# A Strassen-type channel mixer: where its first operands lie, when the right token sums are made, and the order of its last products

## The chip, the cores and the metric

The kernel runs on one core of a Trainium2 chip. The metric is device microseconds (us) of one execution. Engines: PE multiplies matrices, DVE (VectorE), ACT (ScalarE) and POOL (GpSimd) work elementwise, SP issues every transfer of this kernel, in the order of its queue.

## The reference

One layer on 2048 latent tokens of 1024 channels, float32. Up to the middle it is a token mixer (a state-space scan and a pooling mixer, then an output projection); what changes lies behind it:

```
x  = x + mx[2] * rmsnorm(yx, post_norm_mix)
hx = modulate(rmsnorm(x, pre_norm_ffn), mx[3], mx[4])
up = dwconv3(hx @ w_up) ; v, g = split(up)          # 1024 -> 2 x 2816
x  = x + mx[5] * rmsnorm((silu(g) * v) @ w_down, post_norm_ffn)   # 2816 -> 1024
```

## The kernel before, in words

**Numbers.** Each float32 operand is split in two (`split`, lines 117 to 122: `hi` by a cast, line 119, mostly on ACT; `lo = x - hi` by a subtraction, line 122, on DVE or POOL), and each product is three matmuls (`mm3`, lines 150 to 152).

**Token mixer, last part** (lines 906 to 962). The output projection runs over four blocks of 512 tokens, from block 3 down to block 0. Each block takes two halves of the columns; a half needs four units of `w_out` (`wunit`, load at line 129, `lo` on POOL). `Post.half` (lines 810 to 816) squares on ACT (814) and multiplies by the gate row `cr` on DVE (816); `Post.finish` (818 to 836) works out the row scale (`rstd`, lines 154 to 166), loads the residual `xr` (828, two buffers), adds it (834) and stores x1 (836). Blocks 3 and 0 keep their rows in `XB`, blocks 2 and 1 in `eb`. `norm_x1` (880 to 896) then normalises blocks 3, 2 and 1 inside the next block's products and stores them transposed to `h_d` (895): blocks 3 and 2 make the right half of the tokens, `h_d[1]`. Block 0 is done later, by `norm_late`, inside the channel mixer.

**Up-projection** (lines 964 to 1174). It is a Strassen-Winograd product: seven products of quarter matrices in place of eight. `right_sums` (1006) loads four slices of `h_d[1]` (992), makes the sums T1 to T4 (1003) and splits all seven right operands (`xcB11`, `xcT2` and so on) slice by slice. `up_pair(1, i)`, 22 times, loads two units of `w_up` (`rawu`, 1052 and 1057, four buffers), makes weight sums in a buffer `st` (1060 to 1063, two buffers) and runs the products in the order B11, T2, T1, T3, B21, B22, T4, twelve matmuls each, with split weights `wo` (six buffers). Then come the left tokens (`left_sums`, `left_operand`, `up_pair(0, i)`), `act_sums` (sums of the activations, stored to `s_d`, 1146 and 1147) and `down_sums` (sums of `w_down` to `ds_d`).

**Down-projection** (lines 1179 to 1290). Again seven products, of eleven steps each. A step loads a stationary tile `ar` (1200), splits it into `as` (three buffers), loads a weight tile `rw` (1190), splits it into `tc`, and does 24 matmuls on eight banks `psf`. Order: 6, 5, 3, 1, 7, 2, then 4. The last one goes by rows j = 0 to 7, 33 matmuls each. `add` (1241) adds a bank into `accd`; `half_row` squares half a row (1230, ACT) and multiplies it by the gate (1231); `rows` (1211 to 1224) makes the row scales, loads the residual `xr` (1221, two buffers), adds it (1223) and stores the result (1224). Before the change `rows` of both token halves, th = 0 and 1, run inside the last product.

**What sets the order.** Nobody writes the queues by hand: a planner orders each engine's instructions ahead of time. An instruction's rank is its place in the code; `hot()` moves it 500 places ahead. Memory comes from pools that are stacked from the left or the right end and closed together: `sp` (left: `wdt`, `edge`, `tail`, `eb`, `xt`, `ef`, `CT`, `BT` and so on, `cr` near its end) and `main` (right) of the token mixer; `fx` (left) over `sp`, and `fst`, `frw`, `fwo`, `fu` (right) over `main`; at last `fd` (left), 207 KB a partition, over all of these. The channel mixer's pools are opened with `reuse_waits="tile"`.

Of the kernel before, what the change touches and what calls it, by code (L numbers as in the profile page):

```python
# [9 lines left out]
F32 = mybir.dt.float32  # L10
# [25 lines left out]
EPS = 1e-6  # L36


HOT, NW, NPRE, AHEAD, NU, NU2 = 500, 7, 7, 3, 4, 5

ORDER = "p3 c0 p2 c1 p1 b0 p0 b1 x0 x1 x3 x2".split()
ORDER_LAST = "c0 p3 c1 b0 b1 p2 x0 p1 x1 p0 x3 x2".split()
# [10 lines left out]
def hybrid_block(ctx: ExitStack, tc: tile.TileContext, x, cx, ccol, crow, par, rowpar, cst, edge,  # L53
# [3 lines left out]

    const = ctx.enter_context(tc.tile_pool(name="const", bufs=1))
    mctx = ExitStack()
    main = mctx.enter_context(tc.tile_pool(name="main", bufs=1, side="right"))  # L60
    psx, pools = [], {}

# [18 lines left out]
        return main.tile([P, n], F32, tag=name, name=name, bufs=bufs)  # L81

    def t512(dt=F32):
        return main.tile([P, 516], dt, tag="t512", name="t512", bufs=3)

    def cacc():
        return main.tile([P, TB], F32, tag="cacc", name="cacc", bufs=3)

    hxh = main.tile([P, KD, TB + 4], F32R, name="hxh")
    hxl = main.tile([P, KD, TB + 4], F32R, name="hxl")  # L90
# [15 lines left out]
    act_d = [[dp.tile([NK, P, 2 * TB], F32, name=f"act_d{kh}{th}") for th in range(2)] for kh in range(2)]  # L106
    s_d = [dp.tile([NK, P, 2 * TB], F32, name=f"s_d{n}") for n in range(1, 5)]

    hs_d = dp.tile([4, P, 4, TB], F32, name="hs_d")
    ds_d = dp.tile([NK, P, 4, 512], F32, name="ds_d")  # L110
    wu_d = [[dp.tile([P, 1024], F32, name=f"wu_d{m}_{s}") for s in range(4)] for m in range(NFF)]

# [185 lines left out]
    nc.sync.dma_start(out=edge_t, in_=edge.rearrange("g n -> (g n)").partition_broadcast(P))  # L298

    tail = stile([P, 8, 4], "tail")  # L300

    def conv(m, srcs, t, first, dest):


        c0 = 2 if first else 4
        raw = main.tile([P, TB + 4], F32, tag="raw", name="raw", bufs=2)
# [316 lines left out]
    adar = const.tile([P, 32], F32, name="adar")  # L623

    def ada_rest():
        cr = stile([P, D], "cr")
# [250 lines left out]

    A2, B2 = adar[:, 16:24], adar[:, 8:16]

    def norm_x1(ys, b):  # L880

        ss = small(4, "ss4")
        for i in range(4):
            S.activation(out=junk, in_=ys[i], func=AF.Square, accum_out=ss[:, i:i + 1])
        r = rstd(ss, 4, D)
        for i in range(4):
            V.tensor_scalar(out=ys[i], in0=ys[i], scalar1=r[:, i:i + 1], scalar2=None, op0=MUL)
        yield
# [28 lines left out]
    for b in range(NB - 1, -1, -1):  # L917
# [40 lines left out]
            pst.half(hh, po)  # L958
        run(ngen)
        pst.finish()  # L960
        if b:
            ngen = norm_x1(ys, b)
    sctx.close()
# [19 lines left out]
    def four():  # L983
        return fst.tile([P, 4, 512], F32, tag="st", name="st", bufs=2)

    def wide(tag, bufs):
        return main.tile([P, 2 * TB + 4], F32, tag=tag, name=tag, bufs=bufs)

    def quarters_of(p, kk):
        hb = four()  # L990
        for h in range(2):
            nc.sync.dma_start(out=hb[:, 2 * h:2 * h + 2, :],
                              in_=h_d[p][kk + 4 * h].rearrange("p (t c) -> p t c", t=2))
        return hb

    def quarter_sums(hb, put):

        b11, b12, b21, b22 = (hb[:, q_, :] for q_ in range(4))
        for n, s_ in (("B11", b11), ("B21", b21), ("B22", b22)):
            put(n, s_)  # L1000
        for n, o_, x_, y_ in (("T1", b11, b12, b11), ("T3", b12, b22, b12), ("T2", b22, b22, b11),
                              ("T4", b21, b21, b22)):
            V.tensor_tensor(out=o_, in0=x_, in1=y_, op=SUB)  # L1003
            put(n, o_)

    def right_sums():
        for kk in range(4):
            def put(n, s_):
                split(xc[n][:, kk, :], xc[n][:, 4 + kk, :], s_, S, V)
            quarter_sums(quarters_of(1, kk), put)  # L1010

    def left_sums(kk):
        hb = quarters_of(0, kk)
        quarter_sums(hb, lambda n, s_: None)
        nc.sync.dma_start(out=hs_d[:, :, kk, :].rearrange("s p c -> p s c"), in_=hb)

    def left_operand(n):
        hb = four()
        if n in ("T1", "T3", "T4", "T2"):
            src = hs_d[("T1", "T3", "T4", "T2").index(n)]  # L1020
        else:
            h, t = int(n[1]) - 1, int(n[2]) - 1
            src = h_d[0][4 * h:4 * h + 4, :, t * TB:(t + 1) * TB].rearrange("k p c -> p k c")
        nc.sync.dma_start(out=hb, in_=src)
        for h in (0, 2):
            split(xc[n][:, h:h + 2, :], xc[n][:, 4 + h:6 + h, :], hb[:, h:h + 2, :], S, V)

# [127 lines left out]
            V.tensor_tensor(out=o_, in0=x_, in1=y_, op=SUB)  # L1155
        nc.sync.dma_start(out=ds_d[k], in_=t)

    right_sums()
    side = []
    for i in range(4):  # L1160
        side += [norm_late(i)] * 2
    for n_, i in enumerate(j + h * NK for j in range(NK) for h in range(2)):
# [1 line left out]
        if 1 <= n_ <= 8:  # L1164
            next(side[n_ - 1])
        if n_ in (12, 14, 16, 18):
            left_sums(n_ // 2 - 6)
    for n in NAMES:
        left_operand(n)
    for k in range(NK):  # L1170
        vs = [up_pair(0, k)]
        down_sums(k)
# [13 lines left out]
    def weights(n, k):  # L1186

        src = (ds_d if n > 3 else w_down)[k][:, {1: 0, 2: 2, 3: 3, 5: 0, 7: 1, 4: 2, 6: 3}[n], :]
        t = main.tile([P, 512], F32, tag="rw", name="rw", bufs=3)
        nc.sync.dma_start(out=t, in_=src)  # L1190
        tc_ = main.tile([P, 1024], F32R, tag="tc", name="tc", bufs=12)
        split(tc_[:, 0:512], tc_[:, 512:1024], t, S, V)
        return tc_[:, 0:512], tc_[:, 512:1024]

    STAT = {6: s_d[1], 5: s_d[0], 3: s_d[3], 1: act_d[0][0], 7: s_d[2], 2: act_d[1][0], 4: act_d[1][1]}

    def product(n, o, start, stop):
        for k in range(NK):
            t = main.tile([P, 2 * TB], F32, tag="ar", name="ar", bufs=3)
            nc.sync.dma_start(out=t, in_=STAT[n][k])  # L1200
            a = main.tile([P, 2, 2 * TB], F32R, tag="as", name="as", bufs=3)
            split(a[:, 0], a[:, 1], t, S, V)
            w = weights(n, k)
            for j in range(8):
                js = slice(j * P, (j + 1) * P)
# [5 lines left out]
    def rows(th, js):  # L1211
# [49 lines left out]
    product(2, o, True, True)  # L1261
    for j in range(8):
        add(c11, j)
    for j in range(8):
        half_row(3, j)

    tw = [weights(4, k) for k in range(NK)]
    for j in range(8):
        t = main.tile([P, NK, P], F32, tag="ra", name="ra", bufs=2)
        nc.sync.dma_start(out=t, in_=STAT[4][:, :, j * P:(j + 1) * P].rearrange("k p t -> p k t"))  # L1270
        so = main.tile([P, 2, NK, P], F32R, tag="so", name="so", bufs=2)
        split(so[:, 0], so[:, 1], t, S, V)
        if j == 0:
            o = banks()
        for k in range(NK):
            mm3(o[j], (so[:, 0, k, :], so[:, 1, k, :]), tw[k], k == 0, k == NK - 1)
        add(c21, j)
        half_row(2, j)
        if j < 7:
            half_row(0, j)  # L1280
            half_row(1, j)
        if j in (3, 5, 6, 7):
            js = {3: (0, 1, 2, 3), 5: (4, 5), 6: (6,), 7: (7,)}[j]
            rows(1, js)
            if j < 7:
                rows(0, js)
            if j == 6:
                half_row(0, 7)
                half_row(1, 7)
                rows(0, (7,))  # L1290


def _layout(inp):
# [69 lines left out]
```

## Time and profile before

| | us |
|---|---|
| median of 3 runs (lowest, highest) | 2325.04 (2323.08, 2328.54) |
| the profiled execution's own time | 2326.06 |
| its span | 2323.7 |
| PE busy in the span | 2115.2 (91%) |
| DVE, ACT, POOL busy | 1639.1, 904.4, 449.1 |

In time lines the columns are start, duration, engine, source line, operation, output<-input, count and, in brackets, the engine's idle time before it and what ended it. "x2" is two instructions in one row. PEclk 1.00 is full clock (2.4 GHz), 0.50 is 1.2 GHz.

### The profile page before, as it was taken

Reading aid. Unit: us, or ns where it says so; the run is one execution under the profiler, and the core shown is the slowest. Engines: PE = TensorE matmul, PEld = TensorE weight load, DVE = VectorE, ACT = ScalarE, POOL = GpSimd, SP = SyncE. Lnnn points to the kernel's source line nnn. Section 1 sums busy time; section 2 is a strip of 40 time slices with the busy share of each in tenths; the row PEclk is TensorE's granted clock in tenths of the full one; section 3 lists DMA queues with packets and bytes.
Section 4 is the critical chain, followed back from the end, with each engine's and each line's share of the span. In section 5 each row is a group of like instructions: output and inputs, shape, how many; then the busy total and the mean of one; then the engine's idle time right before and its main releaser. Section 6 shows DMA issues by size and latency. Waiting matters only on the chain.

```text
span 2323.7 us, 27270 instructions
## 1 busy us (share of the span) xinstructions
PE 2115.2 (91%) x9473; PEld 1680.8 (72%) x9473; DVE 1639.1 (71%) x2504; ACT 904.4 (39%) x1386; POOL 449.1 (19%) x553
## 2 busy tenths in 40 slices
PE   8788999799789889399999999999999789999994
PEld 4686777687457667188888888877888668888883
DVE  5778868967678565788878888877776643334546
ACT  4434433333324544445544445333333243333331
POOL 1533513525356433000001001100000000000000
PEclk9889999899799889599999999999999989999997
DMA  7757969859765654555576659998867494444417
GB/s 299 269 180 240 310 224 343 271 203 287 243 231 161 221 175 163 212 204 199 209 253 225 248 214 334 384 375 322 281 229 281 156 313 158 147 140 148 141 53 273
DMA packets 238698, 541.37 MB, mean 233 GB/s; under 512 B 52000, under 2 KB 100832, under 8 KB 234720
## 3 DMA queue, kind: packets, MB, share of 16 engines
q1 hardware_dynamic: 238560, 539.64, 66.4%
q8 instruction: 74, 1.21, 0.2%
q14 instruction: 64, 0.52, 0.1%
HBM read 362.22 MB, written 177.34 MB: 232 GB/s over the span
## 4 chain that ended last, share of the span: by engine, by line
PE 53%; DVE 2%; DMA 2%; issue 1%; ACT 1%; SPq 0%; POOL 0%; ACTq 0%; POOLq 0%; DVEq 0%
PE pu L150 12%; PE pu L151 12%; PE pu L152 12%; PE psf L150 6%; PE psf L151 6%; PE psf L152 6%; DMA xr<-x_d 1%; DVE accd L1223 0%; DMA st<-h_d 0%; DVE xcB L122 0%; DMA xr<-in_x_dram 0%; DMA ar<-s_d 0%; DVE st L1003 0%; DVE xcT L122 0%; DVE XB L834 0%
## 5 line engine op out<-in xcount | busy, mean ns | idle before, releaser
L150 PE MATMUL pu<-xcT,wo 128*128 128x512 f32 x704 | 278.4, 396 | 1.3 <-ACT wo L119 1.3
L151 PE MATMUL pu<-xcT,wo 128*128 128x512 f32 x704 | 278.5, 396 | 0.0
L152 PE MATMUL pu<-xcT,wo 128*128 128x512 f32 x704 | 276.9, 394 | 0.0
L150 PE MATMUL pu<-xcB,wo 128*128 128x512 f32 x528 | 210.7, 400 | 40.1 <-ACT xcB L119 36.5
L150 PE MATMUL psf<-tc,as 128*128 128x512 f32 x528 | 204.8, 393 | 21.3 <-ACT tc L119 21.3
L122 DVE TENSOR_TENSOR as<-ar,as 128x1024 fp32r<-128x1024 f32 x66 | 80.8, 1224 | 197.5 <-ACT as L119 197.4
L151 PE MATMUL pu<-xcB,wo 128*128 128x512 f32 x528 | 210.9, 399 | 1.3 <-DVE xcB L122 1.3
L152 PE MATMUL pu<-xcB,wo 128*128 128x512 f32 x528 | 208.6, 398 | 0.0
L151 PE MATMUL psf<-tc,as 128*128 128x512 f32 x528 | 205.7, 389 | 0.0
L152 PE MATMUL psf<-tc,as 128*128 128x512 f32 x528 | 203.1, 389 | 0.0
L150 PE MATMUL pu<-wh,hxh 128*128 128x512 f32 x384 | 157.3, 422 | 23.5 <-DVE eb L816 7.4
L152 PE MATMUL pu<-hxh,wl 128*128 128x512 f32 (+2 forms) x448 | 164.9, 371 | 2.9 <-POOL wl L122 2.0
L150 PE MATMUL pu<-hxh,wh 128*128 128x512 f32 (+2 forms) x448 | 164.8, 373 | 2.0 <-ACT wh L119 1.4
L151 PE MATMUL pu<-hxl,wh 128*128 128x512 f32 (+2 forms) x448 | 166.0, 371 | 0.0
L151 PE MATMUL pu<-wl,hxh 128*128 128x512 f32 x384 | 159.6, 416 | 6.0 <-POOL wl L122 6.0
L122 POOL TENSOR_TENSOR wl<-wst,wh 128x1024 fp32r<-128x1024 f32 x48 | 120.9, 2518 | 217.5 <-ACT wh L119 201.6
L150 PEld LDWEIGHTS pu<-xcT,wo 128*128 128x128 f32 x704 | 132.6, 188 | 33.1 <-ACT wo L119 1.6
L151 PEld LDWEIGHTS pu<-xcT,wo 128*128 128x128 f32 x704 | 132.7, 188 | 31.2
L152 PEld LDWEIGHTS pu<-xcT,wo 128*128 128x128 f32 x704 | 132.4, 188 | 31.1
L119 ACT CAST wo<-rawu 128x512 fp32r<-128x512 f32 x132 | 81.7, 620 | 187.8 <-PE pu L152 168.1
L152 PE MATMUL pu<-wh,hxl 128*128 128x512 f32 x384 | 153.8, 409 | 0.0
L119 ACT CAST as<-ar 128x1024 fp32r<-128x1024 f32 x66 | 69.6, 1054 | 210.4 <-PE psf L152 185.9
(325 smaller groups left out, 4594.6 us busy)
## 6 DMA issues: line engine op xcount, KB each, us to landing
wu_d<-wo SPq DMA_DIRECT2D x88, 512.0 KB, 2.8
wo<-wu_d SPq DMA_DIRECT2D x88, 512.0 KB, 5.7
rawu<-in_w_up_dram SPq DMA_DIRECT2D x66, 512.0 KB, 4.2
wh<-wk_d SPq DMA_DIRECT2D x48, 512.0 KB, 6.7
wl<-wk_d SPq DMA_DIRECT2D x48, 512.0 KB, 6.1
ar<-s_d SPq DMA_DIRECT2D x44, 512.0 KB, 3.4
XB<-in_w_ada_b_dram SPq DMA_DIRECT2D x32, 512.0 KB, 6.7
wst<-in_w_out_dram SPq DMA_DIRECT2D x32, 512.0 KB, 4.4
```

Source lines behind the costliest of these rows:

```text
L119: S.copy(out=hi, in_=src)
L122: le.tensor_tensor(out=lo, in0=src, in1=hi.bitcast(F32), op=ALU.subtract)
L150: PE.matmul(o, lt[0], rt[0], start=start, stop=False, **kw)
L151: PE.matmul(o, lt[0], rt[1], start=False, stop=False, **kw)
L152: PE.matmul(o, lt[1], rt[0], start=False, stop=stop, **kw)
```

## The change

- A new pool `top`, the outermost on the right, takes `t512`, `cacc` and `raw` out of `main`; `frw` (the `rawu` buffers) is the first pool opened on the right afterwards and so lies over `top`. `fst` is gone: its two `st` buffers lie in `fx`. `cr` becomes the fourth tile of `sp`.
- In `fx` the places are given in a new order: B21 and T3 first (over `cr`, `eb`, `xt`), then `st`, then B11, T2, T1. B22 joins T4 in `fu`.
- The quarter sums of the right tokens are made behind block 1 of the output projection, in `XB`, and stored to `hs_d[1]`. The right operands are then loaded whole (1 MB each), as the left ones were, five of them with priority 2000.
- Loads and splits of the down-projection become `hot`; `as` gets two buffers, over the places of B21, allocated ahead of `ar`; its `xr` gets four.
- The products end in the order 6, 5, 3, 2, 1, 7, 4. `half_row` and `rows` for th = 0 move ahead of the adds behind product 7; product 4 keeps those of th = 1.

```diff
@@ pools
-HOT, NW, NPRE, AHEAD, NU, NU2 = 500, 7, 7, 3, 4, 5
+HOT, EARLY, NW, NPRE, AHEAD, NU, NU2 = 500, 2000, 7, 7, 3, 4, 5
+    top = mctx.enter_context(tc.tile_pool(name="top", bufs=1, side="right"))
     main = mctx.enter_context(tc.tile_pool(name="main", bufs=1, side="right"))
...
-        return main.tile([P, 516], dt, tag="t512", name="t512", bufs=3)
+        return top.tile([P, 516], dt, tag="t512", name="t512", bufs=3)
...
-    hs_d = dp.tile([4, P, 4, TB], F32, name="hs_d")
+    hs_d = [dp.tile([4, P, 4, TB], F32, name=f"hs_d{p}") for p in range(2)]
...
     tail = stile([P, 8, 4], "tail")
+    cr = stile([P, D], "cr")
@@ behind block 1
+    def quarter_sums(p, kk, hb):
+
+        for h in range(2):
+            nc.sync.dma_start(out=hb[:, 2 * h:2 * h + 2, :],
+                              in_=h_d[p][kk + 4 * h].rearrange("p (t c) -> p t c", t=2))
+        b11, b12, b21, b22 = (hb[:, q_, :] for q_ in range(4))
+        for o_, x_, y_ in ((b11, b12, b11), (b12, b22, b12), (b22, b22, b11), (b21, b21, b22)):
+            V.tensor_tensor(out=o_, in0=x_, in1=y_, op=SUB)
+        nc.sync.dma_start(out=hs_d[p][:, :, kk, :].rearrange("s p c -> p s c"), in_=hb)
...
         pst.finish()
+        if b == 1:
+            for kk in range(4):
+                quarter_sums(1, kk, XB[:, kk % 2 * 4 * TB:(kk % 2 + 1) * 4 * TB].rearrange("p (q c) -> p q c", q=4))
@@ up-projection
-    fx, fst, frw, fwo = (fpool(*a) for a in (("fx", "left"), ("fst", "right"), ("frw", "right"), ("fwo", "right")))
+    fx, frw, fwo = (fpool(*a) for a in (("fx", "left"), ("frw", "right"), ("fwo", "right")))
...
-    xc = {n: (main if n == "T4" else fx).tile([P, 8, TB], F32R, name="xc" + n) for n in NAMES}
+    def operand(n):
+        xc[n] = (main if n in ("B22", "T4") else fx).tile([P, 8, TB], F32R, name="xc" + n)
+
+    operand("B21")
+    operand("T3")
...
+    sts = [four(), four()]
+    for n in ("B11", "T2", "T1", "B22", "T4"):
+        operand(n)
...
-    def left_operand(n):
-        hb = four()
...
+    def load_operand(p, n):
+        hb = sts.pop() if sts else four()
...
-    right_sums()
+    with tc.high_priority(offset=EARLY):
+        for n in ("B11", "T2", "T1", "T3", "B21"):
+            load_operand(1, n)
+    for n in ("B22", "T4"):
+        load_operand(1, n)
@@ down-projection
-            t = main.tile([P, 2 * TB], F32, tag="ar", name="ar", bufs=3)
-            nc.sync.dma_start(out=t, in_=STAT[n][k])
-            a = main.tile([P, 2, 2 * TB], F32R, tag="as", name="as", bufs=3)
-            split(a[:, 0], a[:, 1], t, S, V)
+            with hot():
+                a = main.tile([P, 2, 2 * TB], F32R, tag="as", name="as", bufs=2)
+                t = main.tile([P, 2 * TB], F32, tag="ar", name="ar", bufs=3)
+                nc.sync.dma_start(out=t, in_=STAT[n][k])
+                split(a[:, 0], a[:, 1], t, S, V)
...
-            res = main.tile([P, D], F32, tag="xr", name="xr", bufs=2)
+            res = main.tile([P, D], F32, tag="xr", name="xr", bufs=4)
...
+    product(2, o, True, True)
+    for j in range(8):
+        S.copy(out=c11[j], in_=o[j])
+    o = banks()
     product(1, o, True, False)
     for j in range(8):
-        S.copy(out=c11[j], in_=o[j])
+        add(c11, j)
         add(c12, j)
     product(7, o, False, True)
+    for js in ((0, 1, 2, 3), (4, 5, 6, 7)):
+        for j in js:
+            half_row(0, j)
+            half_row(1, j)
+        rows(0, js)
     for j in range(8):
+        add(c22, j)
         add(c21, j)
-        add(c22, j)
-    o = banks()
-    product(2, o, True, True)
-    for j in range(8):
-        add(c11, j)
-    for j in range(8):
-        half_row(3, j)
...
             mm3(o[j], (so[:, 0, k, :], so[:, 1, k, :]), tw[k], k == 0, k == NK - 1)
+        half_row(3, j)
         add(c21, j)
         half_row(2, j)
-        if j < 7:
-            half_row(0, j)
-            half_row(1, j)
         if j in (3, 5, 6, 7):
-            js = {3: (0, 1, 2, 3), 5: (4, 5), 6: (6,), 7: (7,)}[j]
-            rows(1, js)
...
+            rows(1, {3: (0, 1, 2, 3), 5: (4, 5), 6: (6,), 7: (7,)}[j])
```

`weights` and the `ra`, `so` tiles of product 4 are put under `hot()` in the same way; `cacc` and `raw` move to `top` like `t512`; `quarter_sums(0, ..)` takes the place of `left_sums`, with the same work.

## Rows read from the trace of the kernel before

**Rows 1.** The page: PE's busy share in 40 slices of the span, in tenths.

```profile
PE   8788999799789889399999999999999789999994
```

**Rows 2.** Windows: stretch, length, busy us (instructions) by engine, PEclk, DMA share, GB/s.

```profile
860.00:900.00 40.00, 39.52 (x176) 31.63 (x175) 25.55 (x44) 22.06 (x41) 14.41 (x6) 1.00 0.56 196
950.00:984.50 34.50, 14.41 (x28) 7.20 (x29) 33.61 (x67) 23.39 (x44) 0.00 (x0) 0.50 0.37 132
1700.00:1800.00 100.00, 100.00 (x432) 80.79 (x431) 70.66 (x78) 31.97 (x40) 8.86 (x27) 1.00 0.76 271
2100.00:2200.00 100.00, 100.00 (x443) 82.81 (x442) 53.17 (x70) 38.02 (x61) 0.00 (x0) 1.00 0.43 143
```

**Rows 3.** Time line of PE: last matmul of block 0, first of the up-projection.

```profile
924.32 0.39 PE L152 MATMUL pu<-wh,hxl 128*128 128x512 f32 x1
949.86 0.79 PE L150 MATMUL pu<-xcB,wo 128*128 128x512 f32 x1 [25.16 <-ACT xcB L119]
```

**Rows 4.** Time line of SP ahead of and around the first handover.

```profile
851.05 6.88 SPq L895 DMA_DIRECT2D h_d<-t  x8
...
916.56 1.69 SPq L895 DMA_DIRECT2D h_d<-t  x2
...
936.81 2.80 SPq L836 DMA_DIRECT2D x_d<-XB  x2
939.71 0.37 SPq L1052 DMA_DIRECT2D rawu<-in_w_up_dram  x1
```

**Rows 5.** Time line of DVE ahead of and around the first handover.

```profile
897.72 0.68 DVE L816 TENSOR_TENSOR XB<-pu,cr 128x512 f32<-128x512 f32 x1
...
928.72 2.48 DVE L834 SCALAR_TENSOR_TENSOR XB<-XB,r,xr 128x1024 f32<-128x1024 f32 x2
...
937.98 1.28 DVE L834 SCALAR_TENSOR_TENSOR XB<-XB,r,xr 128x1024 f32<-128x1024 f32 x1 [1.19 <-DMA xr<-in_x_dram]
```

**Rows 6.** Time line of PE at the second handover.

```profile
1867.79 3.78 PE L150 MATMUL psf<-tc,as 128*128 128x512 f32 x8 [21.28 <-ACT tc L119]
```

**Rows 7.** Time line of SP around the second handover.

```profile
1835.20 19.33 SPq L1128 DMA_DIRECT2D act_d<-av  x2
...
1858.36 1.58 SPq L1147 DMA_DIRECT2D s_d<-av  x2
1860.03 0.58 SPq L1200 DMA_DIRECT2D ar<-s_d  x1
...
1869.51 4.57 SPq L1221 DMA_DIRECT2D xr<-x_d  x2
```

**Rows 8.** Time line: PE's last matmul and DVE's last addition.

```profile
2288.53 0.39 PE L152 MATMUL psf<-tc,so 128*128 128x512 f32 x1
...
2318.60 1.28 DVE L1223 SCALAR_TENSOR_TENSOR accd<-accd,r,xr 128x1024 f32<-128x1024 f32 x1 [2.48 <-DMA xr<-x_d]
```

**Rows 9.** DMA issues, whole span: count, KB each, median us from issue to landing.

```profile
ds_d<-st SPq DMA_DIRECT2D x11, 1024.0 KB, 8.4
...
st<-h_d SPq DMA_DIRECT2D x16, 512.0 KB, 5.1
...
out_dram<-accd SPq DMA_DIRECT2D x16, 512.0 KB, 3.4
```

**Rows 10.** Lines, 940 to 985 us: the sums of the right operands, busy us and mean ns.

```profile
L1003 DVE TENSOR_TENSOR st<-st 128x512 f32<-128x512 f32 x16 | 11.0, 686 | 0.1
```

**Rows 11.** What PE waited for, 690 to 925 us: total, times, longest.

```profile
PE pu L150 <- DVE eb L816: 7.4, 1, 7.4
```

**Rows 12.** Time line of POOL and DVE, 894 to 899 us.

```profile
895.19 2.39 POOL L122 TENSOR_TENSOR wl<-wst,wh 128x1024 fp32r<-128x1024 f32 x1 [5.74 <-PE pu L152]
...
895.35 2.25 DVE L163 TENSOR_TENSOR r<-r 128x4 f32<-128x4 f32 x1
```

**Rows 13.** The page: the split of a 128x1024 tile, `lo` on DVE and `hi` on ACT.

```profile
L122 DVE TENSOR_TENSOR as<-ar,as 128x1024 fp32r<-128x1024 f32 x66 | 80.8, 1224 | 197.5 <-ACT as L119 197.4
...
L119 ACT CAST as<-ar 128x1024 fp32r<-128x1024 f32 x66 | 69.6, 1054 | 210.4 <-PE psf L152 185.9
```

More of the change, by code (lines that the diff above doesn't have):

```diff
@@ L83, in t512 @@
     def t512(dt=F32):
-        return main.tile([P, 516], dt, tag="t512", name="t512", bufs=3)
+        return top.tile([P, 516], dt, tag="t512", name="t512", bufs=3)
     def cacc():
-        return main.tile([P, TB], F32, tag="cacc", name="cacc", bufs=3)
+        return top.tile([P, TB], F32, tag="cacc", name="cacc", bufs=3)
     hxh = main.tile([P, KD, TB + 4], F32R, name="hxh")
@@ L300, in hybrid_block @@
     tail = stile([P, 8, 4], "tail")
+    cr = stile([P, D], "cr")
     def conv(m, srcs, t, first, dest):
         c0 = 2 if first else 4
-        raw = main.tile([P, TB + 4], F32, tag="raw", name="raw", bufs=2)
+        raw = top.tile([P, TB + 4], F32, tag="raw", name="raw", bufs=2)
         if first:
@@ L625, in ada_rest @@
     def ada_rest():
-        cr = stile([P, D], "cr")
         junk2 = stile([P, D], "junk2", 1, BF16)
@@ L972, in fpool @@
         return at.enter_context(tc.tile_pool(name=name, bufs=1, side=side, reuse_waits="tile", **kw))
-    fx, fst, frw, fwo = (fpool(*a) for a in (("fx", "left"), ("fst", "right"), ("frw", "right"), ("fwo", "right")))
+    fx, frw, fwo = (fpool(*a) for a in (("fx", "left"), ("frw", "right"), ("fwo", "right")))
     main = fpool("fu", "right")
     NAMES = ("B11", "T2", "T1", "T3", "B21", "B22", "T4")
-    xc = {n: (main if n == "T4" else fx).tile([P, 8, TB], F32R, name="xc" + n) for n in NAMES}
+    xc = {}
@@ L980, in hybrid_block, with four @@
+    def operand(n):
+        xc[n] = (main if n in ("B22", "T4") else fx).tile([P, 8, TB], F32R, name="xc" + n)
+    operand("B21")
+    operand("T3")
+    def four():
+        return fx.tile([P, 4, 512], F32, tag="st", name="st", bufs=2)
+    sts = [four(), four()]
+    for n in ("B11", "T2", "T1", "B22", "T4"):
+        operand(n)
     sv = main.tile([P, 2 * NFF, 2], F32, name="sv")
     last = main.tile([P, NK], F32, name="last")
-    def four():
-        return fst.tile([P, 4, 512], F32, tag="st", name="st", bufs=2)
@@ L986, in wide @@
     def wide(tag, bufs):
         return main.tile([P, 2 * TB + 4], F32, tag=tag, name=tag, bufs=bufs)
-    def quarters_of(p, kk):
-        hb = four()
[L991 to L1015, printed above, removed]
-    def left_operand(n):
-        hb = four()
-        if n in ("T1", "T3", "T4", "T2"):
-            src = hs_d[("T1", "T3", "T4", "T2").index(n)]
+    def load_operand(p, n):
+        hb = sts.pop() if sts else four()
+        if n[0] == "T":
+            s_ = hs_d[p][("T1", "T3", "T4", "T2").index(n)]
@@ L1021, in left_operand @@
         else:
             h, t = int(n[1]) - 1, int(n[2]) - 1
-            src = h_d[0][4 * h:4 * h + 4, :, t * TB:(t + 1) * TB].rearrange("k p c -> p k c")
-        nc.sync.dma_start(out=hb, in_=src)
+            s_ = h_d[p][4 * h:4 * h + 4, :, t * TB:(t + 1) * TB].rearrange("k p c -> p k c")
+        nc.sync.dma_start(out=hb, in_=s_)
         for h in (0, 2):
@@ L1166, in hybrid_block @@
         if n_ in (12, 14, 16, 18):
-            left_sums(n_ // 2 - 6)
+            quarter_sums(0, n_ // 2 - 6, four())
     for n in NAMES:
-        left_operand(n)
+        load_operand(0, n)
     for k in range(NK):
@@ L1188, in weights @@
         src = (ds_d if n > 3 else w_down)[k][:, {1: 0, 2: 2, 3: 3, 5: 0, 7: 1, 4: 2, 6: 3}[n], :]
[L1189 to L1192, printed above, removed]
+        with hot():
+            t = main.tile([P, 512], F32, tag="rw", name="rw", bufs=3)
+            nc.sync.dma_start(out=t, in_=src)
+            tc_ = main.tile([P, 1024], F32R, tag="tc", name="tc", bufs=12)
+            split(tc_[:, 0:512], tc_[:, 512:1024], t, S, V)
         return tc_[:, 0:512], tc_[:, 512:1024]
@@ L1198, in product @@
         for k in range(NK):
-            t = main.tile([P, 2 * TB], F32, tag="ar", name="ar", bufs=3)
-            nc.sync.dma_start(out=t, in_=STAT[n][k])
-            a = main.tile([P, 2, 2 * TB], F32R, tag="as", name="as", bufs=3)
-            split(a[:, 0], a[:, 1], t, S, V)
+            with hot():
+                a = main.tile([P, 2, 2 * TB], F32R, tag="as", name="as", bufs=2)
+                t = main.tile([P, 2 * TB], F32, tag="ar", name="ar", bufs=3)
+                nc.sync.dma_start(out=t, in_=STAT[n][k])
+                split(a[:, 0], a[:, 1], t, S, V)
             w = weights(n, k)
@@ L1251, in hybrid_block @@
     o = banks()
+    product(2, o, True, True)
+    for j in range(8):
+        S.copy(out=c11[j], in_=o[j])
+    o = banks()
     product(1, o, True, False)
     for j in range(8):
-        S.copy(out=c11[j], in_=o[j])
+        add(c11, j)
         add(c12, j)
     product(7, o, False, True)
+    for js in ((0, 1, 2, 3), (4, 5, 6, 7)):
[3 more added lines that the diff above has]
+        rows(0, js)
     for j in range(8):
+        add(c22, j)
         add(c21, j)
-        add(c22, j)
-    o = banks()
-    product(2, o, True, True)
-    for j in range(8):
-        add(c11, j)
-    for j in range(8):
-        half_row(3, j)
     tw = [weights(4, k) for k in range(NK)]
     for j in range(8):
[L1269 to L1272, printed above, removed]
+        with hot():
+            t = main.tile([P, NK, P], F32, tag="ra", name="ra", bufs=2)
+            nc.sync.dma_start(out=t, in_=STAT[4][:, :, j * P:(j + 1) * P].rearrange("k p t -> p k t"))
+            so = main.tile([P, 2, NK, P], F32R, tag="so", name="so", bufs=2)
+            split(so[:, 0], so[:, 1], t, S, V)
         if j == 0:
@@ L1276, in hybrid_block @@
             mm3(o[j], (so[:, 0, k, :], so[:, 1, k, :]), tw[k], k == 0, k == NK - 1)
+        half_row(3, j)
         add(c21, j)
         half_row(2, j)
-        if j < 7:
-            half_row(0, j)
-            half_row(1, j)
         if j in (3, 5, 6, 7):
-            js = {3: (0, 1, 2, 3), 5: (4, 5), 6: (6,), 7: (7,)}[j]
-            rows(1, js)
[L1285 to L1290, printed above, removed]
+            rows(1, {3: (0, 1, 2, 3), 5: (4, 5), 6: (6,), 7: (7,)}[j])
 def _layout(inp):
```

## The prediction

> **What bounds the kernel now.** The profiled execution took 2326.06 us, with a span of 2323.7; it is the time that the sum is made against, and stands 1.0 above the median of the runs, 2325.04. I read the slices of the page first [rows 1]: from slice 17 on PE is nearly always at nine tenths or more, but for three dips. The windows say that between the dips PE is full and at full clock: 432 matmuls in 100 us of the up-projection, 443 in 100 us of the down-projection, so 0.2315 and 0.2257 us each [rows 2]. There the engines beside PE don't matter. What can be won lies in the dips, and the change works at all three.
>
> First dip, from token mixer to up-projection. The last matmul of block 0 ends at 924.7, the first of the up-projection starts at 949.86 [rows 3]. From 950 to 984.5 PE does 28 instructions, 20 of the first pair's 84 matmuls and 8 transposes, at a granted clock of 0.50, 1.2 GHz, after it had stood still [rows 2]. The other 64 take 64 x 0.2315 = 14.8 us, so the first pair ends at 999.3. Without a dip it would end at 924.7 + 84 x 0.2315 = 944.1. The dip costs 55 us. What was late: the first weights were issued at 939.71, behind the last store of x1 out of `XB` [rows 4], and that store waits for the additions of line 834, the last of them at 937.98 [rows 5]. Then the operands were made slice by slice.
>
> Second dip, into the down-projection: PE waits 21.28 us and does the first eight matmuls in 3.78 us where 1.8 would do [rows 6]: 23 us. SP sat for 19.33 us from 1835.20 in a store of the last pair's result, then stored the four sums, and issued the first `ar` only at 1860.03 [rows 7].
>
> Third, the end: PE stops at 2288.9, DVE's last addition ends at 2319.9, the span at 2323.7 [rows 8]: 34.8 us, in which most of 16 rows still go through two `xr` buffers.
>
> **The change part by part.**
>
> *Right sums behind block 1.* Eight loads, sixteen subtractions and four 1 MB stores move to about 860, when the last block-2 stores of `h_d[1]` are out (851.05 + 6.88 = 857.9) [rows 4]. Two slices fit into `XB` at once. Per round: load 5.1, four subtractions 2.7, store 8.4 us [rows 9, 10]; two rounds are 32 us, and the second slice of each round comes a little later: `XB` is free at about 893 to 900. The first multiplication of block 0 into `XB` was at 897.72 [rows 5]. If it is late, banks stay full and PE waits. The nearest row is such a wait in block 1 before, 7.4 us for L816 [rows 11]. PE was busy for 39.52 of the 40 us from 860 [rows 2], so nothing can be gained there: bounds 0 and 10 (two slices late by 5.1), taken 4. On SP the twelve issues go ahead of `wst`, `xr` and `x_d`, and its queue stands while a store waits for DVE; that is inside the 4.
>
> The sixteen subtractions now run where POOL makes `wl`. While one such POOL instruction of 2.39 us ran, a DVE instruction on 4 columns took 2.25 us [rows 12]. A meeting in each of the four slices would add 4 x 2.3 = 9.2 us to DVE. DVE is busy for 25.55 of those 40 us [rows 2] and has room; what is left of it delays `XB`, within the 10 above. The Trainium skill, page "SBUF — State Buffer", section "Who interferes with whom", says that a VectorE instruction with two SBUF inputs and a GpSimd instruction that reads SBUF take one port in turns, the later one standing still. By that rule the whole 9.2 us would come; without it the subtractions would cost DVE 11 us and no more; the row bears the rule out.
>
> *Weights over `top`.* `rawu` lies over `t512`, `cacc` and `raw` alone. Their last use is behind the last `h_d` store at 918.2 [rows 4], so four loads go out at about 919 in place of 939.7.
>
> *Operands.* B11 and T2 can be loaded behind them, and land by about 930; the sixteen sums (11.0 us [rows 10]) are gone from the dip. But the split weights `wo` lie over `main`, whose last tile is `XB`. I read from both handovers that the planner puts nothing of a new pool into a queue before the pools beneath it are wholly done: `rawu` stood behind the last x1 store though its place had been free for 15 us [rows 3, 4], and `ar` behind the last `s_d` store though all of `fx` was last read before 1846.5 [rows 6, 7]. So the first `wo` stays behind the fourth L834 in DVE's queue. DVE's work from 928.7: four additions of L834, 5.1 [rows 5], three operands by two splits of 1.22, 7.4 [rows 13], and 0.7 for `wo`: 942; with a wait or two I take 943 for the first matmul. Bounds: 940 (the fourth L834 and `wo` alone) and 950 (as now).
>
> From there the first pair needs 19.5 us at full clock. B11 runs at 1.2 GHz, 3 more. The weight sums for T2 need an `st` buffer, and both are held by T1, T3 and B21, which rank higher: a load of 5 to 8 us and a split of 2.4 each, one behind the other in a buffer; I take 4 of waiting there. T4's load is queued behind B22's in the same way: 3. End of the first pair 943 + 19.5 + 3 + 4 + 3 = 972.5. Gain 999.3 - 972.5 = 26.8; less 1 for the eight transposes that now lie between matmuls, less 4 of block 0: **22**, with bounds 8 and 34.
>
> *Early loads of the down-projection.* `as`, `ar` and `hot()` give rank and place, but `fd` lies over all pools of the up-projection, among them `fu`, whose last tiles leave with the `s_d` stores. By the reading above the first `ar` stays behind them: **0**, bounds -2 and 21.
>
> *Two `as` buffers.* A freed buffer is full again after 1.05 + 1.22 = 2.3 us [rows 13], while PE works 24 x 0.2257 = 5.4 us on the other: nothing, with 3.1 us to spare. That room is the cover; the cost without it is a rival below.
>
> *Order 2, 1, 7, 4.* In block 0 it took 4.0 us from the last matmul to the first scaled addition (924.7 to 928.7 [rows 3, 5]), a gate product of 0.7 and the row scale. The end is then an add 0.7, such a stretch 4.0, one addition 1.3 and the 3.8 us from there to the span's end as now [rows 8], in which the store (3.4 to landing [rows 9]) lies: 9.8 in place of 34.8. Against it stands DVE in product 7, which lasts 264 x 0.2257 = 59.6 us: eleven splits of operands and weights (21.0), 16 adds and 16 gate products (0.69 each, 22.0), 8 additions of residuals (10.3) and two row scales (under 3.3 each): 60 us. It just fits; bounds 0 and 8 (one load of `xr` that DVE waits for, with the work behind it), taken 3, paid where the adds free the banks for product 4. Gain 25 - 3 = **22**, bounds 14 and 26 (both late, or a store that lands faster). The th = 0 residuals and results (8 MB) move into product 7's stretch, where DMA was at 0.43 [rows 2].
>
> Sum: 22 + 0 + 22 = 44. 2326 - 44 = 2282, and one less against the median: **2281 us**.
>
> **The rivals.**
>
> That the change does not do what it says is part of the forecast, at the second handover; so the first rival is that it does.
>
> *Both handovers open early* (2240 us). Then `ar` and `wo` come when their own places are free. For it: at 1869.51 SP issued `xr` for the last product [rows 7], so the planner does fetch work from far behind. Against it: the two queues above. It gives a first pair that ends at about 950 to 952, held by T4: 48 - 5 = 43 in the first dip, 20 in the second, 22 at the end: 85.
>
> *The first handover gives nothing* (2303 us): `XB` is late by its full 10 us and the first pair ends at about 989, because T1, T3 and B21 hold both `st` buffers; for it speaks that DVE was busy 33.6 of 34.5 us there [rows 2]. Only the end is won: 22.
>
> *Slower: two `as` buffers are too few* (2347 us). Place: all 66 steps of the down-projection. If adds, gate products and residual additions stand ahead of the split in DVE's in-order queue, a buffer comes back later than 5.4 us. From 3.1 us of such delay on, each us costs 66 us; the gain of 44 is eaten at 3.8 us, and 4.1 us a step gives 66 - 44 = 22 us slower. For it: a product 7 that fills DVE; against it: in the other six products DVE is half idle (53 of 100 us [rows 2]) and the splits rank higher.
>
> **How the numbers follow.** Forecast 0.61, both early 0.14, end only 0.16, slower 0.06; 0.03 for gains and losses that cancel within 0.2%, 4.7 us, which is about what a measurement of this kernel can tell. The range takes the forecast with its bounds (22 to 60 us won: 2265 to 2303), the end-only case, and reaches to the time of both early: 2240 to 2306. It leaves out half of that case, the slower one and the cancelled one, 0.16. Faster by over 0.2%: 0.61 + 0.14 + 0.16 = 0.91; same 0.03; slower 0.06.
>
> **What would show it.** Right: `rawu` issued near 919; the first `wo` split behind the fourth L834, and the first matmul of the up-projection at 940 to 946 on the old clock; the wait before the first `psf` matmul still about 21 us; about 10 us between last matmul and end. Wrong: a wait of a few us there, or a first matmul before 935 (both early); L816 of block 0 late by 10 us and PE idle at about 900 (end only); PE waits on `as` inside the products (slower).

## The result, and the profile after

The changed kernel takes 2301.3 us (median of 4 runs, 2295.74 to 2303.39) against 2324.06 before: a ratio of 0.990, 95% interval 0.987 to 0.992. So 23 us were won where 44 were forecast. The profiled execution took 2301.18 us, with a span of 2298.1, 25.6 less than before.

The page of the changed kernel, PE's busy share in 40 slices, against [rows 1]: the low slice of the first handover (the 17th) rose from 3 to 4 only, the last from 4 to 8; the second handover, a 7 and an 8 before, now falls into one slice, a 6.

```profile
PE   8798999899778788499999999999999969999998
```

The windows of the changed kernel, with the columns of [rows 2]: the stretch in which the right sums are now made, and the first two stretches of 25 us with product 7 in them (it starts at 2160.6).

```profile
860.00:900.00 40.00, 35.64 (x153) 28.27 (x151) 36.03 (x59) 20.18 (x39) 14.02 (x6) 0.96 0.89 313
...
2150.00:2175.00 25.00, 24.43 (x106) 19.32 (x105) 21.09 (x34) 18.15 (x42) 0.00 (x0) 1.00 0.31 95
2175.00:2200.00 25.00, 22.30 (x91) 17.93 (x90) 22.79 (x48) 6.04 (x8) 0.00 (x0) 0.93 0.76 266
```

In the first, PE does 153 instructions where it did 176, and the DMA share rose from 0.56 to 0.89. In the last it does 91 where its full pace is 112.

The time line of PE in the changed kernel, at the places of [rows 3], [rows 6] and [rows 8], with the end of DVE's work in the last line:

```profile
849.74 1.33 PE L903 MATMUL pb<-cs_t,eb 128*128 128x128 f32 x8 [0.94 <-ACT t L905]
...
931.93 0.40 PE L153 MATMUL pu<-wh,hxl 128*128 128x512 f32 x1
953.39 0.80 PE L151 MATMUL pu<-xcB,wo 128*128 128x512 f32 x1 [21.06 <-ACT wo L120]
...
967.99 0.66 PE L1038 MATMUL pb<-cs_t,tt 128*128 128x128 f32 x2 [9.16 <-DVE tt L1031]
...
970.58 0.80 PE L151 MATMUL pu<-xcT,wo 128*128 128x512 f32 x1
...
1837.08 0.39 PE L153 MATMUL pu<-xcT,wo 128*128 128x512 f32 x1
1858.93 0.80 PE L151 MATMUL psf<-tc,as 128*128 128x512 f32 x1 [21.47 <-ACT tc L120]
...
2225.67 0.39 PE L151 MATMUL psf<-tc,so 128*128 128x512 f32 x1
...
2287.29 0.39 PE L153 MATMUL psf<-tc,so 128*128 128x512 f32 x1
...
2293.20 1.29 DVE L1225 SCALAR_TENSOR_TENSOR accd<-accd,r,xr 128x1024 f32<-128x1024 f32 x1
```

From such lines the whole difference can be laid out stretch by stretch. Each stretch runs from the start of one matmul to the start of another:

| Stretch | before, us | after, us | difference |
|---|---|---|---|
| up to the last transposes of block 2's norm | 854.00 | 849.74 | -4.3 |
| to the last matmul of block 0 | 70.3 | 82.2 | **+11.9** |
| to the 84th matmul of the up-projection by count (84 make a pair) | 74.9 | 57.4 | **-17.5** |
| to the last matmul of the up-projection | 846.9 | 847.8 | +0.8 |
| to the first matmul of the down-projection | 21.7 | 21.9 | +0.2 |
| to the first matmul of product 4 | 361.1 | 366.7 | **+5.6** |
| to the last matmul | 59.6 | 61.6 | +2.0 |
| to the span's end | 35.2 | 10.8 | **-24.4** |

The first row is no gain of the change: up to there the engines' orders of work are the same in both kernels. Among the 13 profiled executions of this study that point lies between 846.89 and 854.00, so the stretches behind it are compared from there, not by the clock.

### The profile page after: what moved, and what is told of

Read it like the earlier page. It is cut to its first block, busy times and chain, and to the rows that moved or that the text cites. A ratio compares the mean times of both kernels' runs of the same rounds, so it can differ in the third digit from the quotient of the medians.

```text
span 2298.1 us, 27242 instructions
## 1 busy us (share of the span) xinstructions
PE 2117.2 (92%) x9473; PEld 1684.1 (73%) x9473; DVE 1639.7 (71%) x2464; ACT 902.8 (39%) x1372; POOL 452.1 (20%) x553
## 5 line engine op out<-in xcount | busy, mean ns | idle before, releaser
L151 PE MATMUL pu<-xcB,wo 128*128 128x512 f32 x528 | 210.1, 399 | 25.4 <-ACT wo L120 21.1
L151 PE MATMUL psf<-tc,as 128*128 128x512 f32 x528 | 204.5, 395 | 21.7 <-ACT tc L120 21.5
L152 PE MATMUL psf<-tc,as 128*128 128x512 f32 x528 | 206.0, 390 | 0.0
L151 PE MATMUL pu<-wh,hxh 128*128 128x512 f32 x384 | 156.2, 423 | 29.0 <-DVE eb L817 10.8
L153 PE MATMUL psf<-tc,as 128*128 128x512 f32 x528 | 179.7, 391 | 3.0 <-DVE as L123 3.0
```

The lines of the kernel that those rows point to most:

```text
L151: PE.matmul(o, lt[0], rt[0], start=start, stop=False, **kw)
L152: PE.matmul(o, lt[0], rt[1], start=False, stop=False, **kw)
L153: PE.matmul(o, lt[1], rt[0], start=False, stop=stop, **kw)
```

## The experiments

Each was timed against the kernel before on the same chip. Ratios are to that, with their 95% intervals; the time of the changed kernel in the same form is 0.990 (0.987 to 0.992).

**1. Without the right sums.** `quarter_sums(1, ...)` goes, and the four sums of the right side are filled from plain quarters, so the time is that of a kernel without these sums.

```
-        if b == 1:
-            for kk in range(4):
-                quarter_sums(1, kk, XB[...])
...
-        if n[0] == "T":
+        if n[0] == "T" and p == 0:
```

> Left out: the right token sums (T1 to T4 of the right side are filled from plain quarters). From the last transposes of the block-2 norm to the last matmul of block 0 the kernel before took 70.3 us and the changed one 82.2. Theory (the sums behind block 1 make block 0 late): 70 to 73 us here, and 8 to 12 us less in all, 2289 to 2294. Rival (the lateness is paid back, because the first up-projection matmul hangs on the operand loads): 70 to 73 us as well, but less than 4 us in all, 2298 to 2302.

Measured: 2289.8 us, ratio 0.985 (0.983 to 0.987), and 70.0 us from the transposes (850.37) to the last matmul of block 0 (920.38). The theory holds for block 0: the sums behind block 1 cost 12.2 us there. How much of that stays in the total is less sure: 11.5 us by the medians, 10 by the ratios, and 7.4 from the transposes to the last matmul of the two profiled executions, because the next stretch, to the 84th matmul, takes 61.7 us here and 57.4 in the changed kernel. So a part, up to 4 us, is paid back there, which the rival had for nearly all of it. The windows of this kernel over the same 40 us:

```profile
860.00:900.00 40.00, 39.83 (x182) 32.05 (x181) 28.81 (x49) 21.90 (x41) 16.34 (x7) 1.00 0.59 204
```

PE is full again, with the DMA share back at 0.59.

**2. The sums' transfers without the subtractions.** The eight loads and four stores stay, the sixteen subtractions go.

```
-        for o_, x_, y_ in (...):
+        for o_, x_, y_ in (...) if p == 0 else ():
             V.tensor_tensor(out=o_, in0=x_, in1=y_, op=SUB)
```

> Left out: the sixteen subtractions of the right sums; their eight loads and four stores stay. Theory A (the subtractions hold DVE, beside POOL, and DVE holds the banks): as without the sums, 70 to 74 us from the transposes to the last matmul of block 0, total within 2 us of that kernel. Theory B (SP's queue and the transfers: the weight loads stand behind the stores of the sums): 79 to 82 us, total within 3 us of the changed kernel, 2298 to 2304.

Measured: 79.7 us for the stretch (851.53 to 931.22), and a total of 2297.6 us, ratio 0.989 (0.987 to 0.991). That is theory B's side: of 12.2 us, 9.7 are there without one subtraction. The windows of this kernel:

```profile
860.00:900.00 40.00, 33.04 (x141) 24.97 (x140) 22.44 (x38) 18.19 (x32) 11.88 (x5) 0.99 0.97 352
```

B named two things at once, SP's queue and the transfers; the next run tries to part them.

**3. The same transfers through ScalarE's queue**, again without the subtractions.

```
-            nc.sync.dma_start(out=hb[...], in_=h_d[p]...)
+            (S if p else nc.sync).dma_start(out=hb[...], in_=h_d[p]...)
...
-        nc.sync.dma_start(out=hs_d[p]..., in_=hb)
+        (S if p else nc.sync).dma_start(out=hs_d[p]..., in_=hb)
```

> Left out: the sixteen subtractions of the right sums, as in the kernel without them; their eight loads and four stores go through ScalarE's queue, so that SP's is free of them. That kernel took 79.7 us from the transposes to the last matmul of block 0, and 70.0 without the sums' transfers. Theory (8 MB of transfers fill the DMA engines and the weights land late): 77 to 82 us again. Rival (the weight loads stand in SP's queue behind stores that wait): 70 to 74 us.

Measured: 81.3 us (848.43 to 929.71), ratio 0.988 (0.986 to 0.990). With SP's queue free of the sums' transfers the weights of block 0 were no earlier. The windows of this kernel, and what ScalarE waited for between 850 and 932 us (total, times, longest):

```profile
860.00:900.00 40.00, 31.67 (x131) 24.32 (x130) 23.75 (x40) 16.13 (x30) 11.63 (x5) 0.91 0.95 345
```

```profile
ACT wh L120 <- DMA wst<-in_w_out_dram: 12.2, 3, 6.1
```

The DMA engines are busy for 0.95 of the time, and the casts of the weights wait for their loads. The loads of `w_out` issued between 855 and 905 us (count, KB each, median us to landing), in the kernel before, the changed one, run 2 and this run:

```profile
wst<-in_w_out_dram SPq DMA_DIRECT2D x7, 512.0 KB, 4.7
wst<-in_w_out_dram SPq DMA_DIRECT2D x6, 512.0 KB, 4.3
wst<-in_w_out_dram SPq DMA_DIRECT2D x6, 512.0 KB, 6.7
wst<-in_w_out_dram SPq DMA_DIRECT2D x6, 512.0 KB, 6.6
```

Without the subtractions a load takes 2 us longer than before, whichever queue has the sums' transfers. But the queue isn't ruled out. SP stood in this run for 15.9 us of the same stretch, 10.8 at the longest, in stores of x1 that waited for DVE (6.6 before), with loads of weights behind them; and ScalarE's own waits for the sums' loads may have added to the delay here, which they can't have in the run before. What SP waited for, before and in this run:

```profile
SPq L836 <- DVE eb L834: 6.6, 4, 3.1
SPq L837 <- DVE eb L835: 15.9, 4, 10.8
```

The Trainium skill, page "DMA: Bandwidth & Descriptors", section "Issuing engines are not separate DMA queues", says that transfers started from different engines end up on the same 16 DMA engines and interleave. The traces agree: the 40 us from 860 moved 345 GB/s at a DMA share of 0.95 here, and 352 at 0.97 with everything on SP's queue (run 2).

**4. Three buffers for `as`, two for `xr`**, as before the change, everything else as changed.

```
-                a = main.tile([P, 2, 2 * TB], F32R, tag="as", name="as", bufs=2)
+                a = main.tile([P, 2, 2 * TB], F32R, tag="as", name="as", bufs=3)
...
-            res = main.tile([P, D], F32, tag="xr", name="xr", bufs=4)
+            res = main.tile([P, D], F32, tag="xr", name="xr", bufs=2)
```

> Theory (two buffers for the stationary operand are what stalls PE in product 7): with three, PE's loss there of 6 us against 112 matmuls per 25 us falls under 1 us; with two xr buffers in place of four the tail grows by 0 to 3 us; total 2295 to 2300. Rival (adds and gate products stand ahead of the splits in DVE's queue, and three buffers don't cover it): the loss stays at 4 to 6 us and the total is 2300 to 2305. Product 4: 0.227 us per matmul if the place of the tiles set the 0.234, 0.234 if the order of the products did.

Measured: 2292.7 us, ratio 0.986 (0.985 to 0.988), below the range expected. From the first matmul of the down-projection to product 4 it takes 360.7 us in place of 366.7: the loss of 6.1 us is that of having two buffers. It lies in product 7: the 27 matmuls that the two windows of the changed kernel lack are 6.0 us, and PE waits for `as` nowhere else. Its windows there:

```profile
2150.00:2175.00 25.00, 25.00 (x112) 20.72 (x111) 21.50 (x34) 16.85 (x41) 0.00 (x0) 1.00 0.28 95
2175.00:2200.00 25.00, 25.00 (x112) 20.69 (x111) 20.02 (x47) 9.37 (x13) 0.00 (x0) 1.00 0.76 261
```

DVE is as crowded, but PE never falls under 112. How the two buffers lost it shows in DVE's and PE's time lines of the changed kernel:

```profile
2173.67 3.69 DVE L1233 TENSOR_TENSOR accd<-accd,gate 128x512 f32<-128x512 f32 x6
2177.29 1.21 DVE L123 TENSOR_TENSOR as<-ar,as 128x1024 fp32r<-128x1024 f32 x1
```

```profile
2178.56 1.88 PE L153 MATMUL psf<-tc,as 128*128 128x512 f32 x6 [2.70 <-DVE as L123]
2179.59 1.70 PE L153 MATMUL psf<-tc,as 128*128 128x512 f32 x4
2181.09 0.63 PE L151 MATMUL psf<-tc,as 128*128 128x512 f32 x1
```

The split of the next `as` stands behind six gate products, PE waits 2.70 us, and then goes on at 0.43 us a matmul for a while: the granted clock of that window is 0.93. The tail, 10.6 us here, doesn't miss the two `xr` buffers. On product 4 this run could not answer: it keeps 0.2343 us a matmul, but an `as` of 8 KB more and two `xr` of 4 KB less leave `so` where it was.

**5. The new order of the end alone**, put into the kernel before.

```
-    product(1, o, True, False)
-    ...
-    product(7, o, False, True)
-    ...
-    product(2, o, True, True)
+    product(2, o, True, True)
+    ...
+    product(1, o, True, False)
+    ...
+    product(7, o, False, True)
+    ...
```

> The kernel before with the new order of the end alone (three buffers for the stationary operand, two for xr, no priorities). Theory: the tail behind the last matmul falls from 35.2 to 11 to 14 us and product 7 loses under 1 us: 20 to 24 us less than before, 2300 to 2304. Rival (the crowded product 7 takes its toll with three buffers too): 15 to 18 us less, 2306 to 2309.

Measured: 2302.5 us, ratio 0.991 (0.989 to 0.993), 20.7 less than before on that chip; the tail is 10.8 us (last matmul 2287.14, span 2297.9), and PE is full in product 7. So the order alone gives about as much as the whole change, and the rest of the change, with its two `as` buffers and its right sums, comes out at about nothing.

**6. A pool of its own for the down-projection's operands**, over the place of `fx` alone. From here on the experiments start from the kernel with three `as` buffers.

```
-    main = fpool("fd", "left", ctx)
+    fe, main = fpool("fe", "left", ctx), fpool("fd", "left", ctx)
...
-            t = main.tile([P, 512], F32, tag="rw", name="rw", bufs=3)
+            t = fe.tile([P, 512], F32, tag="rw", name="rw", bufs=3)
```

(and `tc`, `as` and `ar` likewise)

> On top of the kernel with three stationary buffers: the tiles for stationary operands and weights of the down-projection in a pool of their own, over the place of fx alone. Theory (the planner holds a new pool's work back until the pools beneath are wholly done, and so the first ar sits in SP's queue behind the last act_d and s_d stores): the first ar is issued before the act_d store that sits 19 us, and PE's wait before the first psf matmul falls from 21.7 to 3 to 8 us; 13 to 18 us less than the 2293 of that kernel, 2275 to 2280. Rival (banks or the sums of the last pair are late anyway): a wait of 15 us or more, 2286 to 2293.

Measured: 2273.6 us, ratio 0.977 (0.975 to 0.979): 19 us less than with three buffers alone, more than expected. SP's time line of this kernel, and PE's:

```profile
1826.26 0.32 SPq L1203 DMA_DIRECT2D ar<-s_d  x1
...
1846.97 0.32 SPq L1124 DMA_DIRECT2D act_d<-av  x1
```

```profile
1834.09 0.40 PE L153 MATMUL pu<-xcT,wo 128*128 128x512 f32 x1
1834.32 0.39 PE L151 MATMUL psf<-tc,as 128*128 128x512 f32 x1
```

The first `ar` goes out 21 us ahead of the store that it stood behind, and there is no wait at all between the two projections. Not all of the 21.8 us stays won: up to product 4 the down-projection takes 365.0 us in place of 360.7, since PE now waits for the copies of the first product's banks, and the granted clock of the 25 us around that wait is 0.86:

```profile
1897.21 0.79 PE L151 MATMUL psf<-tc,as 128*128 128x512 f32 x1 [2.86 <-ACT accd L1246]
```

**7. The first pair's weight sums third.** The loads of `rawu` and the four weight sums of the first pair become a function of their own, which is called behind the loads of B11 and T2.

```
         for n in ("B11", "T2", "T1", "T3", "B21"):
             load_operand(1, n)
+            if n == "T2":
+                pre.append(up_weights(1, 0))
```

> On top of three stationary buffers: the weight sums of the first up-projection pair take the st buffer after B11 and T2, ahead of T1, T3, B21, B22 and T4. Theory (the sums stood behind six operand loads in two buffers, and T2's product with them): from the first up-projection matmul to the first of T2's at most 8 us in place of 17; the first matmul itself as late as before, about 21 us behind block 0; 6 to 10 us less, 2283 to 2287. Rival (the operands behind the sums are late instead): the first pair ends no earlier, 2290 to 2294.

Measured: 2287.5 us, ratio 0.983 (0.982 to 0.985). The first matmul comes 21.6 us behind block 0, as before, but T2's first matmul 1.0 us after it in place of 16.2 to 17.2; the 84th is 45.7 us behind block 0 in place of 55.9 (with three buffers) and 57.4. So about 10 us of that dip were the `st` ring: the sums took their turn behind six operands. In all it gives 5 us, against 2292.7 on another chip (7 by the ratios). A part of the rest is lost further on: from the 84th matmul to the last of the up-projection it takes 850.7 us in place of 847.0, with two waits for operands (0.3 and 1.5 us) right behind the 84th, where the kernel of run 4 has none.

**8. The weights' ring in a pool of its own**, on top of the run before, so that `fwo` lies over no tile of the x1 rows.

```
-    main = mctx.enter_context(tc.tile_pool(name="main", bufs=1, side="right"))
+    mw, main = (mctx.enter_context(tc.tile_pool(name=n_, bufs=1, side="right")) for n_ in ("mw", "main"))
...
-                st = main.tile([P, 1024], F32, tag="w", name="wst", bufs=NW)
+                st = mw.tile([P, 1024], F32, tag="w", name="wst", bufs=NW)
```

> As the kernel with the sums third, and the ring of the token mixer's weights in a pool of its own, so that the first wo lies over no tile of the x1 rows. Theory (the pool boundary alone keeps the first wo behind T1's split on ACT and the fourth row addition on DVE): the first up-projection matmul comes 8 to 12 us behind the last of block 0 in place of 21, and 14 to 20 us less than the 2293 of three buffers, 2273 to 2279. Rival (something else holds wo): still about 21 us, and the time of the kernel with the sums third.

Measured: 2285.0 us, ratio 0.982 (0.980 to 0.985). ScalarE's time line of the changed kernel, then PE's of this one:

```profile
936.86 1.99 ACT L120 CAST xcT<-st 128x1024 fp32r<-128x1024 f32 x2 [0.48 <-DMA st<-hs_d]
948.28 1.99 ACT L120 CAST xcT<-st 128x1024 fp32r<-128x1024 f32 x2 [9.43 <-DMA st<-hs_d]
950.83 1.99 ACT L120 CAST xcT<-st 128x1024 fp32r<-128x1024 f32 x2 [0.55 <-DMA st<-hs_d]
952.73 0.61 ACT L120 CAST wo<-rawu 128x512 fp32r<-128x512 f32 x1
```

```profile
931.36 0.40 PE L153 MATMUL pu<-wh,hxl 128*128 128x512 f32 x1
935.15 0.80 PE L151 MATMUL pu<-xcB,wo 128*128 128x512 f32 x1 [3.38 <-ACT xcB L120]
939.92 0.79 PE L152 MATMUL pu<-xcB,wo 128*128 128x512 f32 x1 [3.98 <-DVE xcB L123]
...
946.98 0.50 PE L151 MATMUL pu<-xcT,wo 128*128 128x512 f32 x1 [2.19 <-ACT wo L120]
```

The mechanism is as the theory had it: the first matmul now comes 3.8 us behind block 0, sooner than the 8 to 12 expected. The price is not: 2.5 us less than the run before, with overlapping intervals, where about 9 were expected (between the middles of the two expected ranges). Started earlier, PE waits for the operands one by one, and the 84th matmul is 44.3 us behind block 0, 1.4 sooner than without the pool.

**9. Three together** (6, 7 and 8 on three `as` buffers).

> Three stationary buffers, the own pool for the down-projection's operands, the sums third and the weights' ring in its own pool, together. Theory (they work at different places): 2273.6 of the own pool less the 7.7 that the sums third and the ring gave, 2264 to 2268. Rival (what comes earlier up-stage waits again down-stage): 2270 to 2275.

Measured: 2262.2 us, ratio 0.974 (0.972 to 0.976), a little under the range expected and better than both kernels of this study: 39 us under the changed one.

**10. Half of the right sums later**, in block 1's `eb` tiles behind its norm, on top of the three.

```
-            for kk in range(4):
-                quarter_sums(1, kk, XB[...])
+            for kk in (0, 1):
+                quarter_sums(1, kk, XB[...])
...
+        if b == 0:
+            for kk in (2, 3):
+                quarter_sums(1, kk, stile([P, 2 * D], "eb", 2)...)
```

> As the three together, with the second half of the right sums moved behind block 1's norm, into its eb tiles. Theory (transfers make block 0 late): 74 to 77 us from the transposes to the last matmul of block 0 in place of 82.8; the second operand comes up to 5 us later behind block 0; 3 to 7 us less than the three together. Rival (the late half holds T2 by as much): within 2 us of the three together.

Measured: 2268.1 us, ratio 0.976 (0.974 to 0.977): worse than the three if anything, where 3 to 7 us less, or by the rival the same time, was expected. Block 0 took 74.4 us, as the theory of the transfers says, but the first up-projection matmul waits 22 us again. Its time lines of SP and PE:

```profile
926.69 4.54 SPq L889 DMA_DIRECT2D hs_d<-eb  x2
...
938.11 1.02 SPq L1023 DMA_DIRECT2D st<-h_d  x1
```

```profile
947.60 0.79 PE L151 MATMUL pu<-xcB,wo 128*128 128x512 f32 x1 [22.13 <-ACT xcB L120]
```

B11's load comes behind the late stores. `fx` lies over the pool of `eb`, so the pool boundary of run 6 would explain it; that was not tried by itself.

**11. `so` allocated ahead of `xr`**, on top of the three.

```
             half_row(0, j)
+            if j == 0:
+                ra_so = (main.tile([P, NK, P], ...), main.tile([P, 2, NK, P], ...))
             half_row(1, j)
```

> As the three together, with so and ra allocated ahead of xr, so that so lies where the kernel before had it. Theory (the place of so sets the pace): 0.227 us per matmul in product 4 and 1 to 2 us less in all. Rival (the order of the products does): 0.233 to 0.235 as in the kernels with the new order, and the same time.

Measured: 2262.3 us, ratio 0.973 (0.972 to 0.974), the same; product 4 goes at 0.2324 us a matmul, against 0.2333 with the three and 0.2267 before. So this place isn't what slows it; what does stays open (2 us in all).

## Why the prediction was right and where it was not

The direction was right and the time lies in the range, but it is nearly the time of a rival, "the first handover gives nothing" (2303), and that in part by chance. The rival has 0 for the first dip and 22 for the end; the runs show 5.6 (17.5 won, 11.9 lost) and 16.8. One of its two reasons, a late `XB`, did not happen; the other, the operands that hold both `st` buffers, did. The forecast itself had 22 for each.

**Block 0, taken as 4 with 10 as its bound, was 11.9 us late.** I costed the moved sums by latency, a load of 5.1, subtractions of 2.7, a store of 8.4, and asked only when `XB` comes free. `XB` did come in time: its first multiplication ran at 898.20. The weights of block 0 came late, and by runs 1 and 2 the sums' transfers are 9.7 of the 12.2 us. Two terms of theirs were wrong. I gave the traffic no price: eight loads of 512 KB and four stores of 1 MB are 8 MB; at the 345 GB/s of run 3 that is 24 us of all DMA engines, put into a stretch whose share was 0.56 [rows 2] and then was 0.89. And SP's queue, which I took to be inside the 4, stood for 12.0 us in the four stores, which waited for the subtractions (SP in the changed kernel, 855 to 905 us):

```profile
SPq L889 <- DVE XB L888: 12.0, 4, 4.5
```

In the changed kernel itself this second term shows most plainly: by the median a load of `w_out` lands as soon after its issue as before (4.3 us against 4.7; the slowest took 9.6 against 7.4), but the fifth one is issued 41.1 us behind the transposes in place of 32.6. In run 2 the subtractions are gone; there the loads take 6.7 us to land, and SP stands for 12.5 us in the sums' own loads and stores, which wait for each other. How the delay divides between queue and traffic stays open: run 3 doesn't part them.

On the subtractions the meetings with POOL came about as reckoned, three in place of four (min, median and longest ns of the sixteen):

```profile
L888 DVE TENSOR_TENSOR XB<-XB x16: 676/684/2889, 861.4 to 891.7; 128x512 f32<-128x512 f32 x16
```

Thirteen took 676 to 695 ns; the three that ran while POOL made a `wl` took 1.40, 2.78 and 2.89 us, 5 us more in all where I had 9.2. This is the rule of the Trainium skill, page "SBUF — State Buffer", section "Who interferes with whom" (DVE and GpSimd take a shared port in turns), and the trace agrees. It changed the time little: all sixteen together are 2.5 us of the 12.2 by run 2.

**The first handover gave 17.5, not 26.8.** My reading that a new pool's work waits for the pools beneath was right; run 8 shows it for `wo` and run 6 for `ar`. `rawu` was issued at 923.07, block 0 being late. The terms that failed are what stands between and the turn in the `st` ring. Of the 9.6 us that the stretch to the 84th matmul is longer than forecast (57.4 against 972.5 - 924.7), 2.8 lie ahead of the first matmul, which comes at 953.39 after 21.1 us where 18.3 were forecast, and 6.8 behind it. I let the first `wo` wait for the row additions and three operands, up to 943; it stood on ScalarE's queue behind the casts of T1 and T3 as well, whose loads were issued only at 941 and landed 7 us later. And for the weight sums' turn in the `st` ring I took 4 us, and run 7 shows about 10. That the 84th matmul came at 989.3, where the rival has 989, is luck in part: this execution was 4.3 us ahead before the change begins.

**The second handover, forecast at 0**, was 0: 21.9 us against 21.7. `hot()` on `ar` did nothing here: rank doesn't pass the pool boundary, as run 6 shows, which left the rank and changed the pool. It also shows what was there to be had: 19 us.

**The end gave 16.8 us, not 22.** The tail was right, 10.8 against 9.8. "Two `as` buffers: nothing" was wrong: the room of 3.1 us a step holds in the other five products with an `as`, and fails in product 7, where adds and gate products stand ahead of the split. I had that mechanism as a rival over all 66 steps and didn't carry it to the one product that I had myself called full. With the 3 taken for a crowded DVE against 5.6 measured it looks like a small miss, but run 4 shows that the crowd alone costs nothing. Product 4's slower pace, 2.0 us, I had not foreseen.

## What to carry to other kernels

Cost moved transfers by their bytes and by the queue they stand in, too: where a stretch has little DMA room left, or a store waits at the head of an in-order queue, transfers that nobody waits for make late the ones that somebody does. Before giving a buffer away, look for the stage in which the engine that refills it is fullest; an average over the stage says nothing. And where a planner orders a new pool's work behind the whole of the pools under it, place decides and rank doesn't: put what the next stage needs first over what the last stage frees first.

## What the runs showed that was not expected

Product 4 has two paces with the clock granted in full: 0.2267 us a matmul in the kernel before and 0.2324 to 0.2343 in every kernel with the new order, from its first matmul to its last. Its cause is open.

The point in the trace that no edit here touches, the last transposes of block 2's norm, lay up to 7 us apart between executions (846.89 to 854.00), as much as several of the effects told above; so two profiles have to be compared stretch by stretch.
